# Two transformer stacks on one core: high and low activation parts side by side in one 512-column product

## The chip, the cores and the metric

The kernel runs on one core of one Trainium2 chip, as one program. The metric is the device time of one execution in microseconds. Before the change the median of three runs is 2209.1 us (2205.93 to 2218.09).

## What is computed

The input is one sequence of 256 tokens with 1024 features. Block 1 is two hybrid layers and a final norm, block 2 is two layers with a context of 256 more tokens. Everything is float32.

```python
def hybrid_layer(x, ...):                     # block 1, twice
    h = rms_norm(x, norm_mix)
    proj = h @ w_in                           # 1024 x 10032: all queries, keys, values, gates
    y_nsa, y_sb, y_gla, y_fox = ...           # sparse, stick-breaking, gated linear, forgetting attention
    branch = einsum('bsnc,ncd->bsnd', stack(ys), w_branch)
    gates = sigmoid(gate_logits + b_gate)
    x = x + sum(gates * branch) @ w_out
    h2 = rms_norm(x, norm_ff)
    return x + square(relu(h2 @ w_ff1)) @ w_ff2

# block 2, for each of two layers, modulated by c:
x = layer_norm(alpha * x + g_a * mixer(...))  # layer 0: grouped queries; layer 1: latent attention
x = layer_norm(alpha * x + g_m * square(relu(h @ w1)) @ w2)
```

In the last layer of block 2 only the 256 tokens of x are computed, not the context.

## The kernel before

Activations lie feature by token: x is [128, 8, 256], eight blocks of 128 features by 256 tokens. To keep float32 accuracy with the fast float32r products, each operand is split into a high part (rounded to float32r) and a low part (the rest). A product is then three: high·high, high·low, low·high (mm3, line 348). Weights are loaded by SyncE in tiles of [128, 1024] words (load, 354; five buffers raw), split on ScalarE (cast to hi) and VectorE (subtraction to lo) (split, 359; four buffers each of hi and lo) and used once.

fm8 (372) computes 256 output features for all tokens, a "chunk": for each of two halves of 128 features it loads one weight tile and issues eight triples mm3, k = 0 to 7, with the weights as the stationary operand and 256 columns of xh or xl as the moving one, into one half of a PSUM tile g ([128, 2, 256], one bank, three of them). It is used for the projections of block 1 (16 chunks besides the gates), its gates (16), its output projection (4) and ff1 (16), in each of the two layers. tm8 (381) is the same with tokens as output rows.

layer1 (510) is one layer of block 1. norm_in (721) multiplies x by the norm's gain and splits it into xh and xl; the row scale 1/rms (rc per token, rb broadcast over the partitions) comes later from sumsq (726) and is multiplied in on VectorE as each chunk leaves PSUM (lines 557 to 656, rope 1017) or on ScalarE (tm_evac, 743). branch (569) computes gates and branch projections of one mixer. gla_attn (866) is the gated linear attention: for each half of the tokens t and each pair of heads pr it forms decayed keys xe and queries xq for eight levels and multiplies them per head, with 64 rows of the array (one head has 64 features), into PSUM tiles attps; copy_predicated writes them into att under the masks glm. glq and glk share a tile glqk.

The feed-forward of a layer runs 16 chunks: ff1 (684) with fm8, ReLU, square and split into hid; ff2 (694) adds two rows of 128 hidden features to eight accumulators acc, one chunk behind. When the last row is through, r2b scales each acc and it is added to x. In the second half of the loop of the last layer, at chunk 11, the pool of block 1 on the right side (br) is closed and the one of block 2 opened; context_in (1663) loads the context xc into it and casts its normed parts. VectorE also computes the modulation vectors of block 2 in this loop (ada, 1173).

mlp256 (1518) is the last feed-forward of block 2, on 256 tokens, with the split input hh, hl of two tiles H ([128, 8, 512], of which the tokens use one half); up projection in triples of 256 columns, hidden (1484), and one row of the down projection per step, two steps behind. ln_last (1255) and the output follow.

SBUF has pools on two sides: bp, scp and the weight buffers on the left, br (tags Y, tm, cst and others; for block 2 xc, cst2, H) on the right, where x lies too. Tiles of one tag rotate through its buffers (tag A: 11, tag Y: nY = 3, each of 2048 words per partition). Within a pool the tags lie in the order of their first use.

The order of the instructions on each engine is not the order of the code. The program is built with a planner (TileContext with schedule_with_timeline_sim) that places each instruction by estimated times as its operands and buffers come free. An instruction waits on its engine's queue in that order.

Of the kernel before, what the change touches and what calls it, by code (L numbers as in the profile page):

```python
# [26 lines left out]
BR_ORDER = (1, 2, 0, 3)  # L27

# [278 lines left out]

class Prog:
# [43 lines left out]


# [27 lines left out]
    def tm8(self, src, j, xh, xl):  # L381
# [3 lines left out]
        for t in range(2):  # L385
            s = slice(t * 128, t * 128 + 128)
            for k in range(8):
                h, q = parts[k // 4]
                self.mm3(ps[:, t, :], xh[:, k, s], xl[:, k, s], h[:, k % 4, :], q[:, k % 4, :], k == 0, k == 7)
# [120 lines left out]
    def layer1(self, l):  # L510
# [21 lines left out]
        for j in range(4):  # L532
            h, q = self.split(self.tm_raw[j] if l == 0 else self.load(I[f"wtm{l}"][j], 2, TM_W))
            for t in range(2):
                o = pst[t][:].rearrange("p a b -> p (a b)")[:, :TM_W]
                s = slice(t * 128, t * 128 + 128)
                for k in range(2):
                    kk = j * 2 + k
                    self.mm3(o, xh[:, kk, s], xl[:, kk, s], h[:, k, :], q[:, k, :], kk == 0, kk == 7)
# [16 lines left out]
        for j in range(2):  # L556
            ps = self.fm8(win, C_SBQ + j, xh, xl)
            self.stt(sbq[:, 2 * j:2 * j + 2, :], ps[:], 0.125, rbb, OP.mult, OP.mult)
        for j in range(2):
            ps = self.fm8(win, C_SBK + j, xh, xl)  # L560
            self.tt(sbk[:, 2 * j:2 * j + 2, :], ps[:], rbb, OP.mult)
        for j in range(2):
            self.tm_evac(sbv, j, self.tm8(win, C_SBV + j, xh, xl), rc)
# [1224 lines left out]
```

## Time and profile before

| | us |
|---|---|
| median of three runs | 2209.1 |
| the profiled execution | 2211.48 |
| its span | 2209.8 |
| TensorE busy | 2135.6 (97%) |
| VectorE busy | 1518.5 (69%) |
| ScalarE busy | 1069.7 (48%) |
| GpSimd busy | 132.7 (6%) |

Block 1 takes the first 1211 us or so (layer 0 until about 605), block 2 the rest; mlp256 begins at about 2004 us. TensorE executes 15024 products and as many weight loads. A float32 product that is not float32r is recorded as two passes. Matmuls are pipelined and each row's duration reaches beyond the start of the next, so the price of a product is read from the distance of two starts. In tables of groups the columns are: line, engine, operation, output and inputs by tile names, shape, count, then busy us and mean ns of one, then the idle time before them and what ended it.

### The profile page before, as it was taken

The numbers are of one execution on the slowest core, as the hardware profiler recorded it, in microseconds if no ns is written. First come the engines' busy times: TensorE is split into PE (matmuls) and PEld (weight loads), VectorE is DVE, ScalarE is ACT, GpSimd is POOL, SyncE is SP. The second block draws the span as 40 slices with busy tenths as digits, with TensorE's granted clock in tenths as the row PEclk, the third lists the DMA queues.
The fourth block names the chain that finished last, engine by engine and source line by source line (L and its number), as shares of the span: only waits on it lengthen the run. The fifth ranks groups of instructions, "written<-read, shape, count | busy, mean of one in ns | idle before, by whom it ended". The sixth has DMA issues, their size and how long they took to land. (4 is left out here: it accounts for less than half of the span.)

```text
span 2209.8 us, 37629 instructions
## 1 busy us (share of the span) xinstructions
PE 2135.6 (97%) x15024; PEld 1912.2 (87%) x15024; DVE 1518.5 (69%) x2859; ACT 1069.7 (48%) x1773; POOL 132.7 (6%) x151
## 2 busy tenths in 40 slices
PE   8999999999999999999999899999999999998998
PEld 8889889999998898899999776878888888578997
DVE  6586766788664767677887677479866456756554
ACT  5633554555555335555465477352322325655443
POOL 1100000000001000000000111210000041000000
PEclk9999999999999999999999999999999999999999
DMA  7343334588654433356787110127765322124652
GB/s 264 126 177 117 125 116 159 185 271 275 223 163 125 172 118 127 112 171 188 261 299 235 63 30 29 58 77 219 253 204 178 98 77 76 50 74 132 185 183 77
DMA packets 94388, 335.35 MB, mean 152 GB/s; under 512 B 10722, under 2 KB 12420, under 8 KB 94212
## 3 DMA queue, kind: packets, MB, share of 16 engines
q1 hardware_dynamic: 94212, 332.95, 46.7%
q8 instruction: 118, 1.93, 0.4%
q14 instruction: 58, 0.48, 0.1%
HBM read 331.85 MB, written 1.05 MB: 151 GB/s over the span
## 5 line engine op out<-in xcount | busy, mean ns | idle before, releaser
L321 ACT ACTIVATE hi<-raw 128x1024 fp32r<-128x1024 f32 (+2 forms) x510 | 534.5, 1050 | 754.4 <-PE g L338 242.3
L324 DVE TENSOR_TENSOR lo<-raw,hi 128x1024 fp32r<-128x1024 f32 (+2 forms) x510 | 626.8, 1231 | 312.0 <-ACT hi L321 308.9
L338 PE MATMUL g<-xh,lo 128*128 128x256 f32 x1024 | 294.4, 288 | 0.8 <-DVE lo L324 0.8
L338 PE MATMUL g<-xh,hi 128*128 128x256 f32 x1024 | 295.1, 288 | 0.1
L338 PE MATMUL g<-xl,hi 128*128 128x256 f32 x1024 | 295.1, 288 | 0.0
L338 PE MATMUL acc<-hid,hi 128*128 128x256 f32 x1536 | 278.6, 284 | 2.7 <-ACT hi L321 1.5
L338 PEld LDWEIGHTS acc<-hid,hi 128*128 128x128 f32 x1536 | 237.6, 193 | 3.9 <-ACT hi L321 2.1
L1186 DVE CUSTOM_DVE_ANT_0 sc<-raw,sc 128x1024 f32<-128x1024 f32 x160 | 195.2, 1220 | 49.0 <-DMA raw<-wada 48.7
L338 PE MATMUL acc<-hid,lo 128*128 128x256 f32 x768 | 210.8, 285 | 2.1 <-DVE lo L324 2.0
L338 PEld LDWEIGHTS g<-xh,hi 128*128 128x128 f32 x1024 | 196.3, 192 | 10.4 <-issue 7.9
L338 PEld LDWEIGHTS g<-xl,hi 128*128 128x128 f32 x1024 | 196.2, 192 | 6.4 <-issue 5.5
L338 PEld LDWEIGHTS g<-xh,lo 128*128 128x128 f32 x1024 | 196.4, 192 | 5.3 <-issue 2.7
L338 PE MATMUL gu<-hl,hi 128*128 128x256 f32 (+1 forms) x608 | 196.1, 327 | 1.1 <-DVE hl L332 1.1
L338 PE MATMUL gu<-hh,lo 128*128 128x256 f32 (+1 forms) x608 | 196.2, 328 | 0.5 <-DVE lo L324 0.5
L338 PE MATMUL gu<-hh,hi 128*128 128x256 f32 (+1 forms) x608 | 187.2, 327 | 3.0 <-ACT relu L321 1.9
L338 PEld LDWEIGHTS acc<-hid,lo 128*128 128x128 f32 x768 | 144.7, 193 | 3.6 <-DVE lo L324 3.5
L338 PE MATMUL g<-fh,lo 128*128 128x256 f32 x512 | 145.0, 283 | 0.7 <-DVE lo L324 0.7
L338 PE MATMUL g<-fl,hi 128*128 128x256 f32 x512 | 145.1, 284 | 0.0
L338 PE MATMUL g<-fh,hi 128*128 128x256 f32 x512 | 144.7, 283 | 0.0
L338 PE MATMUL m<-hid,hi 128*128 128x512 f32 x464 | 142.7, 389 | 0.0
L338 PEld LDWEIGHTS gu<-hl,hi 128*128 128x128 f32 x608 | 115.0, 189 | 13.4 <-DVE hl L332 2.1
L338 PEld LDWEIGHTS gu<-hh,lo 128*128 128x128 f32 x608 | 115.0, 189 | 10.9 <-DVE lo L324 0.7
(440 smaller groups left out, 4330.5 us busy)
## 6 DMA issues: line engine op xcount, KB each, us to landing
raw<-win SPq DMA_DIRECT2D x152, 512.0 KB, 3.5
raw<-wff SPq DMA_DIRECT2D x128, 512.0 KB, 4.6
raw<-wada SPq DMA_DIRECT2D x96, 512.0 KB, 4.5
raw<-w1m SPq DMA_DIRECT2D x64, 512.0 KB, 4.3
raw<-w2m SPq DMA_DIRECT2D x64, 512.0 KB, 4.2
raw<-wbr SPq DMA_DIRECT2D x32, 512.0 KB, 3.4
raw<-wc SPq DMA_DIRECT2D x16, 512.0 KB, 3.6
raw<-wout SPq DMA_DIRECT2D x16, 512.0 KB, 3.4
```

The lines of the kernel that those rows point to most:

```text
L321: return self.nc.scalar.activation(out, in_, func, bias=bias, scale=scale)
L324: return self.nc.vector.tensor_tensor(out=out, in0=a, in1=b, op=op)
L338: i = self.nc.tensor.matmul(out, lhsT, rhs, start=start, stop=stop, skip_group_check=True)
L1186: self.nc.vector.tensor_tensor_reduce(out=sc[2][:], in0=w, in1=sc[v][:], op0=OP.mult, op1=OP.add, scale=0.5, scalar=0.0, accum_out=mod[:, ...
```

## The change

A pair tile holds the high and the low part of an activation block next to each other ([128, 4, 2, 256], two tiles of tag Y for all eight blocks). One product of 512 columns then gives weight-high times both parts, and one of 256 columns adds weight-low times the high part to the second half (mm2). The two halves of the PSUM tile are added as they leave (add2: a ScalarE copy of one half, a VectorE addition of the other). fm8 yields one half of 128 features at a time, each in a PSUM tile of its own. This holds for all chunks of block 1 and for the up projection of mlp256.

After the row scale is known a second pair xn = x · gain · rb is formed, and all projections after SBQ and SBK take it, so that the multiplication by rb goes there. In gla_attn the queries of a pair of heads lie side by side in 256 columns with zeros in the other head's rows, so that one product of 128 rows serves both heads; the predicated copies cover both heads too. glk gets a tile of tag Y of its own, nY becomes 5, and the old tiles xh, xl go. The last three rows of the feed-forward's down projection (in both layers of block 1 and in mlp256) run inside one loop over the eight output blocks, so that the accumulators end one after the other. The output projection adds the two halves to x one by one.

```diff
+class Pair:
+    def __init__(self, tiles):
+        self.t = tiles
+    def both(self, k):
+        return self.t[k // 4][:, k % 4]
+    def part(self, j, k, s=slice(0, T)):
+        return self.t[k // 4][:, k % 4, j, s]
+    def two(self, j, k):
+        return self.t[k // 4][:, k % 4:k % 4 + 2, j, :]
...
+    def mm2(self, ps, lh, ll, both, hi, start, stop):
+        self.mm(ps, lh, both, start, False)
+        self.mm(ps[:, 1, :], ll, hi, False, stop)
+    def add2(self, out, ps):
+        self.act(out, ps[:, 1, :])
+        return self.tt(out, out, ps[:, 0, :], OP.add)
...
-    def fm8(self, src, j, xh, xl):
-        ps = self.gtile()
+    def fm8(self, src, j, X):
         for f in range(2):
+            ps = self.gtile()
             h, q = self.split(self.load(src[2 * j + f], 8, 128))
             for k in range(8):
-                self.mm3(ps[:, f, :], h[:, k, :], q[:, k, :], xh[:, k, :], xl[:, k, :], k == 0, k == 7)
-        return ps
...
-        xh = self.bp.tile([128, 8, T], F32R, tag="xh", name="xh", bufs=1)
-        xl = self.bp.tile([128, 8, T], F32R, tag="xl", name="xl", bufs=1)
+        xg = self.pair("xg")
         col = self.psp.tile([128, 512], F32, tag="o", name="ncol", bufs=1)
-        self.norm_in(x, v("gmix"), xh, xl)
+        self.norm_in(x, v("gmix"), xg)
...
-            ps = self.fm8(win, C_SBQ + j, xh, xl)
-            self.stt(sbq[:, 2 * j:2 * j + 2, :], ps[:], 0.125, rbb, OP.mult, OP.mult)
+            s = slice(2 * j, 2 * j + 2)
+            self.fm8_to(sbq[:, s, :], win, C_SBQ + j, xg)
+            self.stt(sbq[:, s, :], sbq[:, s, :], 0.125, rbb, OP.mult, OP.mult)
...
+        xn = self.pair("xn")
+        for k in range(0, 8, 2):
+            t = self.scp.tile([128, 2, T], F32, tag="tmp", name="xnt", bufs=2)
+            for f in range(2):
+                self.stt(t[:, f, :], x[:, k + f, :], v("gmix")[:, k + f:k + f + 1], rb[:], OP.mult, OP.mult)
+            self.act(xn.two(0, k), t[:])
+            self.tt(xn.two(1, k), t[:], xn.two(0, k).bitcast(F32), OP.subtract)
         for j in range(2):
-            self.tm_evac(sbv, j, self.tm8(win, C_SBV + j, xh, xl), rc)
+            self.tm_evac(sbv, j, self.tm8(win, C_SBV + j, xn))
...
-                ps = self.fm8(win, C_GATE + bi * 4 + j, xh, xl)
+                g = gt[-1][:, 2 * (j % 2):2 * (j % 2) + 2, :]
+                for f, ps in self.fm8(win, C_GATE + bi * 4 + j, xn):
+                    self.add2(g[:, f, :], ps)
+                    self.tanh(g[:, f, :], g[:, f, :], hb[:, bi * 8 + 2 * j + f:bi * 8 + 2 * j + f + 1], 0.5)
                 step()
-                g = gt[-1][:, 2 * (j % 2):2 * (j % 2) + 2, :]
-                self.tt(g, ps[:], rbb, OP.mult)
-                for f in range(2):
-                    self.tanh(g[:, f, :], g[:, f, :], hb[:, bi * 8 + 2 * j + f:bi * 8 + 2 * j + f + 1], 0.5)
...
-        glqk = self.a4([128, 2, 2, T], name="glqk")
-        glq, glk = glqk[:, 0], glqk[:, 1]
-        ps = self.fm8(win, C_GLQ, xh, xl)
-        self.stt(glq, ps[:], 0.125, rbb, OP.mult, OP.mult)
-        ps = self.fm8(win, C_GLK, xh, xl)
-        self.tt(glk, ps[:], rbb, OP.mult)
+        glq = self.a4([128, 2, 2, T], name="glq")
+        for h in range(2):
+            nc.gpsimd.memset(glq[64 * (1 - h):64 * (1 - h) + 64, :, h, :], 0.0)
+        tq = self.scp.tile([128, 2, T], F32, tag="tmp", name="glqt", bufs=2)
+        self.fm8_to(tq, win, C_GLQ, xn)
+        for h in range(2):
+            s = slice(64 * h, 64 * h + 64)
+            self.act(glq[s, :, h, :], tq[s], scale=0.125)
+        glk = self.y8([128, 2, T], name="glk")
+        self.fm8_to(glk, win, C_GLK, xn)
...
-        mh = self.y8([128, 8, T], F32R, name="mh")
-        ml = self.y8([128, 8, T], F32R, name="ml")
+        mx = self.pair("mx")
...
-            ps = self.fm8(I[f"wout{l}"], j, mh, ml)
-            self.tt(x[:, 2 * j:2 * j + 2, :], x[:, 2 * j:2 * j + 2, :], ps[:], OP.add)
+            for f, ps in self.fm8(I[f"wout{l}"], j, mx):
+                for e in range(2):
+                    self.tt(x[:, 2 * j + f, :], x[:, 2 * j + f, :], ps[:, e, :], OP.add)
...
-        fh = self.bp.tile([128, 8, T], F32R, tag="xh", name="fh", bufs=1)
-        fl = self.bp.tile([128, 8, T], F32R, tag="xl", name="fl", bufs=1)
+        fx = self.pair("fx")
...
-            ps = self.fm8(I[f"wff1{l}"], ci, fh, fl)
             hid = self.a4([128, 2, 2, T], F32R, name="hid")
             t = self.scp.tile([128, 2, T], F32, tag="tmp", name="relu", bufs=2)
-            self.act(t[:], ps[:], AF.Relu)
+            self.fm8_to(t, I[f"wff1{l}"], ci, fx)
+            self.act(t[:], t[:], AF.Relu)
...
+                if 2 * ci + k < 32 - LAST:
+                    ff2_rows([(2 * ci + k, hid)], lambda f: None)
+        def ff2_rows(rows, done):
+            ws = [(r, hid, self.split(self.load(I[f"wff2{l}"][r], 1, 1024))) for r, hid in rows]
+            for f in range(8):
+                s = slice(f * 128, f * 128 + 128)
+                for r, hid, (h, q) in ws:
+                    self.mm3(acc[f // 2][:, f % 2, :], h[:, 0, s], q[:, 0, s], hid[:, 0, r % 2, :], hid[:, 1, r % 2, :],
+                             r == 0 and f % 2 == 0, r == 31)
+                done(f)
+        def ff_out(f):
+            if f % 2 == 1:
+                j = f // 2
+                t = self.scp.tile([128, 2, T], F32, tag="tmp", name="ffo", bufs=2)
+                self.tt(t[:], acc[j][:], r2bb, OP.mult)
+                self.tt(x[:, 2 * j:2 * j + 2, :], x[:, 2 * j:2 * j + 2, :], t[:], OP.add)
...
+        ff2_rows([(r, hids[r // 2]) for r in range(32 - LAST, 32)], ff_out)
...
+    def pair(self, name):
+        return Pair([self.y8([128, 4, 2, T], F32R, name=name) for _ in range(2)])
...
-                xq = self.a4([128, 8, 128], name="xq")
+                xq = [self.a4([128, 4, 2, 128], name="xq") for _ in range(2)]
                 for hf in range(2):
                     ps = self.psp.tile([128, 512], F32, tag="t", name="eps", bufs=2)
                     w = self.glw[:, t + 4 * hf:t + 4 * hf + 4, :]
...
                     self.mm(ps[:], la_l[:, t, pr * 128:pr * 128 + 128], w, False, True)
                     x4 = slice(4 * hf, 4 * hf + 4)
                     self.act(xe[:, x4, :], ps[:].rearrange("p (a b) -> p a b", a=4), AF.Exp)
-                    self.tt(xq[:, x4, :], xe[:, x4, :], glq[:, pr, ts_].unsqueeze(1).broadcast_to([128, 4, 128]), OP.mult)
+                    self.tt(xq[hf][:], xe[:, x4, :].unsqueeze(2).broadcast_to([128, 4, 2, 128]),
+                            glq[:, pr, :, ts_].unsqueeze(1).broadcast_to([128, 4, 2, 128]), OP.mult)
                 self.tt(xe[:], xe[:], glk[:, pr, ts_].unsqueeze(1).broadcast_to([128, 8, 128]), OP.mult)
-                for lq in range(2):
-                    ps = [self.psp.tile([128, 4, 128], F32, tag="s", name="attps", bufs=2) for _ in range(2)]
-                    for lj in range(4):
-                        li = 4 * lq + lj
-                        for h in range(2):
-                            s = slice(h * 64, h * 64 + 64)
-                            if li == 0:
-                                self.mm(ps[h][:, lj, :], glk[s, pr, ts_], glq[s, pr, ts_])
-                            else:
-                                self.mm(ps[h][:, lj, :], xe[s, slot(li), :], xq[s, slot(li), :])
-                    for lj in range(4):
-                        for h in range(2):
-                            nc.vector.copy_predicated(att[:, 2 * pr + h, :], self.glm[:, 4 * lq + lj, :], ps[h][:, lj, :])
+                for lp in range(4):
+                    ps = self.psp.tile([128, 2, 2, 128], F32, tag="s", name="attps", bufs=2)
+                    for lj in range(2):
+                        li = 2 * lp + lj
+                        if li == 0:
+                            self.mm(ps[:, lj], glk[:, pr, ts_], glq[:, pr, :, ts_])
+                        else:
+                            self.mm(ps[:, lj], xe[:, slot(li), :], xq[slot(li) // 4][:, slot(li) % 4])
+                    for lj in range(2):
+                        nc.vector.copy_predicated(att[:, 2 * pr:2 * pr + 2, :],
+                                                  self.glm[:, 2 * lp + lj, :].unsqueeze(1).broadcast_to([128, 2, 128]),
+                                                  ps[:, lj])
                 if t == 0:
                     self.act(xk0[:, pr, :], xe[:, 0, :])
                 else:
-                    ps = [self.psp.tile([128, 128], F32, tag="s", name="attx", bufs=2) for _ in range(2)]
-                    for h in range(2):
-                        s = slice(h * 64, h * 64 + 64)
-                        self.mm(ps[h][:], xk0[s, pr, :], xq[s, 7, :])
-                    for h in range(2):
-                        self.act(att0[:, 2 * pr + h, 128:256], ps[h][:])
+                    ps = self.psp.tile([128, 2, 128], F32, tag="s", name="attx", bufs=2)
+                    self.mm(ps[:], xk0[:, pr, :], xq[1][:, 3])
+                    self.act(att0[:, 2 * pr:2 * pr + 2, 128:256], ps[:])
...
-            self.nA, self.nY = 11, 3
+            self.nA, self.nY = 11, 5
...
+        def rows(js, done):
+            ws = [(i, hids[i], self.split(self.load(self.i["w2m1"][i], 1, 1024))) for i in js]
+            for f in range(8):
+                w = slice(f * 128, f * 128 + 128)
+                for i, hid, (h, q) in ws:
                     self.mm3(acc[f // 2][:, f % 2, :], h[:, 0, w], q[:, 0, w], hid[:, 0, :T], hid[:, 1, :T],
                              i == 0 and f % 2 == 0, i == 31)
-        for f in range(8):
-            self.stt(X[:, f, s], acc[f // 2][:, f % 2, :], mod[:, 40 + f, 0:1], X[:, f, s], OP.mult, OP.add)
+                done(f)
...
+        def up(ps, k, h, q):
+            self.mm2(ps[:], h[:, k, :], q[:, k, :], hx[:, k], hx[:, k, 0, :], k == 0, k == 7)
...
+            self.add2(t[:, :T], ps)
+            self.stt(t[:, T:], t[:, :T], 0.0, t[:, :T], OP.max, OP.mult)
+            self.act(o[:, 0, :T], t[:, T:])
+            self.tt(o[:, 1, :T], t[:, T:], o[:, 0, :T].bitcast(F32), OP.subtract)
...
+            if 3 <= j < 35 - LAST:
+                rows([j - 3], lambda f: None)
+        rows(range(32 - LAST, 32), out)
...
-            hh, hl = self.w16(name="hh"), self.w16(name="hl")
+            hx = self.w16(name="hx")[:].rearrange("p k (a t) -> p k a t", a=2)
```

## Rows read from the trace of the kernel before

**Rows 1.** The page: busy time by engine; granted TensorE clock in 40 slices.
```profile
PE 2135.6 (97%) x15024; PEld 1912.2 (87%) x15024; DVE 1518.5 (69%) x2859; ACT 1069.7 (48%) x1773; POOL 132.7 (6%) x151
PEclk9999999999999999999999999999999999999999
```
**Rows 2.** Busy time of each engine by stage: stretch, length, then us busy.
```profile
60.00:430.00 370.00, 367.90 (x2871) 334.67 (x2870) 255.39 (x547) 183.17 (x329) 14.46 (x25) 1.00 0.42 139
430.00:603.00 173.00, 171.69 (x1423) 170.79 (x1422) 139.58 (x198) 90.20 (x109) 0.00 (x0) 1.00 0.77 258
...
2016.00:2190.00 174.00, 173.60 (x1448) 173.61 (x1449) 94.37 (x125) 80.23 (x122) 0.00 (x0) 1.00 0.54 167
```
**Rows 3.** TensorE in order of time, a projection: start, length, instruction.
```profile
59.82 0.28 PE L338 MATMUL g<-xh,hi 128*128 128x256 f32 x1
...
60.18 0.28 PE L338 MATMUL g<-xh,hi 128*128 128x256 f32 x1
```
**Rows 4.** TensorE in order of time, the first down projection of block 2.
```profile
1500.05 0.39 PE L338 MATMUL m<-hid,lo 128*128 128x512 f32 x1
...
1500.73 0.39 PE L338 MATMUL m<-hid,lo 128*128 128x512 f32 x1
```
**Rows 5.** TensorE in order of time, the first up projection of block 2.
```profile
1480.07 0.40 PE L338 MATMUL gu<-hh,hi 128*128 128x512 f32 x1
...
1480.77 0.40 PE L338 MATMUL gu<-hh,hi 128*128 128x512 f32 x1
```
**Rows 6.** Groups of instructions: high·high products of the projections and of ff1.
```profile
L338 PE MATMUL g<-xh,hi 128*128 128x256 f32 x1024 | 295.1, 288 | 0.1
...
L338 PE MATMUL g<-fh,hi 128*128 128x256 f32 x512 | 144.7, 283 | 0.0
```
**Rows 7.** Groups of instructions on VectorE and, last, ScalarE.
```profile
L324 DVE TENSOR_TENSOR lo<-raw,hi 128x1024 fp32r<-128x1024 f32 x494 | 612.3, 1241 | 301.3 <-ACT hi L321 298.5 <-PE g L338 0.8
...
L901 DVE COPY_PREDICATED att<-glm,attps 128x128 f32<-128x128 uint8 x128 | 36.6, 300 | 19.3 <-PE attps L338 17.2
...
L324 DVE TENSOR_TENSOR gt<-g,rb 128x512 f32<-128x512 f32 x32 | 21.9, 688 | 10.1 <-PE g L338 9.9
...
L324 DVE TENSOR_TENSOR xq<-xe,glqk 128x512 f32<-128x512 f32 x16 | 10.5, 686 | 0.1
...
L332 DVE SCALAR_TENSOR_TENSOR fnt<-x,lngb,fncol 128x256 f32<-128x256 f32 x8 | 3.6, 476 | 1.8 <-PE fncol L338 1.8
...
L324 DVE TENSOR_TENSOR yns<-nso,yns 128x256 fp32r<-128x256 f32 x8 | 3.4, 425 | 7.2 <-ACT yns L321 7.2
...
L321 ACT ACTIVATE yns<-nso 128x256 fp32r<-128x256 f32 x8 | 3.1, 384 | 10.1 <-PE nso L338 10.1
```
**Rows 8.** TensorE in order of time, two stretches of the gated linear attention.
```profile
144.67 1.71 PE L338 MATMUL attps<-xq,xe 64*128 64x128 f32 x16
...
151.42 0.28 PE L338 MATMUL g<-xh,hi 128*128 128x256 f32 x1
151.62 0.49 PE L338 MATMUL attps<-glqk 64*128 64x128 f32 x2
...
152.93 0.28 PE L338 MATMUL g<-xh,lo 128*128 128x256 f32 x1
```
**Rows 9.** A sum of squares on TensorE: in order of time, and as a group.
```profile
1221.24 1.03 PE L338 MATMUL fncol<-fsq,ones 128*128 128x256 f32 x4
...
L338 PE MATMUL fncol<-fsq,ones 128*128 128x256 f32 x8 | 2.1, 379 | 0.0
```
**Rows 10.** TensorE in order of time, where layer 1 of block 1 begins.
```profile
606.35 0.41 PE L338 MATMUL g<-hi,xh 128*128 128x304 f32 x1 [1.08 <-ACT xh L321]
```
**Rows 11.** The context's tile xc: instructions with first and last start, and landing.
```profile
L321 ACT ACTIVATE ct<-xc,mod x8: 586/587/601, 1149.3 to 1156.7; 128x256 f32<-128x256 f32 x8
...
L1670 SPq DMA_DIRECT2D xc<-ctxT x2: 372/398/424, 1143.9 to 1144.3; - x2
...
DMA to landing us min/median/max: 5.3/6.3/7.4
```

More of the change, by code (lines that the diff above doesn't have):

```diff
@@ L27 @@
 BR_ORDER = (1, 2, 0, 3)
+LAST = 3
 def _cols(w, kt, cw):
@@ L370, in gtile, with fm8_to, tm8 @@
         return self.psp.tile([128, 2, 256], F32, tag="g", name="g", bufs=3)
-    def fm8(self, src, j, xh, xl):
-        ps = self.gtile()
+    def fm8(self, src, j, X):
         for f in range(2):
+            ps = self.gtile()
             h, q = self.split(self.load(src[2 * j + f], 8, 128))
             for k in range(8):
-                self.mm3(ps[:, f, :], h[:, k, :], q[:, k, :], xh[:, k, :], xl[:, k, :], k == 0, k == 7)
-        return ps
-    def tm8(self, src, j, xh, xl):
+                self.mm2(ps[:], h[:, k, :], q[:, k, :], X.both(k), X.part(0, k), k == 0, k == 7)
+            yield f, ps[:]
+    def fm8_to(self, dst, src, j, X):
+        for f, ps in self.fm8(src, j, X):
+            self.add2(dst[:, f, :], ps)
+    def tm8(self, src, j, X):
         ps = self.gtile()
@@ L695, in ff2 @@
             for k in range(2):
[L696 to L702 removed]
+                if 2 * ci + k < 32 - LAST:
[14 more added lines that the diff above has]
+                self.tt(x[:, 2 * j:2 * j + 2, :], x[:, 2 * j:2 * j + 2, :], t[:], OP.add)
+        prev, hids = None, []
         ada = self.ada(0, [self.a4([128, D], name="sc") for _ in range(3)], range(24 * l, 24 * l + 24))
@@ L741, in sumsq, with tm_evac @@
         return self.diag(col, 2)
-    def tm_evac(self, dst, j, ps, rc):
-        for t in range(2):
-            self.act(dst[:, t, j * 256:j * 256 + 256], ps[:, t, :], AF.Identity, scale=rc[:, t:t + 1])
+    def tm_evac(self, dst, j, ps):
+        self.act(dst[:, :, j * 256:j * 256 + 256], ps[:])
     def set_ln(self):
@@ L1516, in mlp512, with mlp256 @@
                         lambda k: (hid[k][:, 0, :], hid[k][:, 1, :]), toks, lambda f, *a: evac(5 + f, *a), done)
-    def mlp256(self, X, hh, hl, mod, s):
+    def mlp256(self, X, hx, mod, s):
         acc = [self.psp.tile([128, 2, T], F32, tag=("s" if j < 2 else "t"), name="acc2", bufs=2) for j in range(4)]
         hids = []
-        first = self.fmu_first([self.i["w1m1"][e] for e in range(3)], hh, hl, [s])
-        for j in range(34):
-            if j < 32:
-                hids.append(self.hidden(first[j] if j < 3 else self.fmu(self.i["w1m1"][j], 8, hh, hl, s), T))
-            if j >= 2:
-                i, hid = j - 2, hids[j - 2]
-                h, q = self.split(self.load(self.i["w2m1"][i], 1, 1024))
-                for f in range(8):
-                    w = slice(f * 128, f * 128 + 128)
+        def rows(js, done):
[3 more added lines that the diff above has]
+                for i, hid, (h, q) in ws:
@@ L1530, in mlp256, with out @@
                     self.mm3(acc[f // 2][:, f % 2, :], h[:, 0, w], q[:, 0, w], hid[:, 0, :T], hid[:, 1, :T],
                              i == 0 and f % 2 == 0, i == 31)
-        for f in range(8):
-            self.stt(X[:, f, s], acc[f // 2][:, f % 2, :], mod[:, 40 + f, 0:1], X[:, f, s], OP.mult, OP.add)
+                done(f)
+        def out(f):
+            if f % 2 == 1:
+                for e in (f - 1, f):
+                    self.stt(X[:, e, s], acc[e // 2][:, e % 2, :], mod[:, 40 + e, 0:1], X[:, e, s], OP.mult, OP.add)
@@ new lines, in mlp256 @@
+        pss = [self.gtile() for _ in range(3)]
+        ws = [self.split(self.load(self.i["w1m1"][e], 8, 128)) for e in range(3)]
+        for k in range(8):
+            for ps, (h, q) in zip(pss, ws):
+                up(ps, k, h, q)
+        for j in range(32):
+            if j < 3:
+                ps = pss[j]
+            else:
+                ps = self.gtile()
+                h, q = self.split(self.load(self.i["w1m1"][j], 8, 128))
+                for k in range(8):
+                    up(ps, k, h, q)
+            hid(ps[:])
+            if 3 <= j < 35 - LAST:
+                rows([j - 3], lambda f: None)
```

70 lines of the change are left out of this document (34 added, 36 removed).

## The prediction, made before the changed kernel ran

> **What bounds the kernel now.** I read the page's busy shares first. TensorE is busy 97% of the span, at full granted clock in every fortieth of it [rows 1]. That share is modelled, so I went to the table by stage. The mixer part of layer 0 (60 to 430 us) has TensorE busy 367.9 of 370 us, its feed-forward part (430 to 603 us) 171.7 of 173, the last MLP (2016 to 2190 us) 173.6 of 174, while VectorE is at 69%, 81% and 54% and ScalarE below that [rows 2]. Layer 1 of block 1 repeats the first two. So in the stages that the change touches only the time that TensorE needs per product counts, unless the edits make another engine late.
>
> The order of TensorE's work then tells the price of one product. In a projection the three products of a triple (256 columns each, each with its own weight load) take 0.36 us, 120 ns each, with no wait between [rows 3]. Products of 512 columns show two prices in the second block. Those of the first down projection, whose moving operand lies in the left-hand pool, take 0.68 us for three, 227 ns each [rows 4]. Those of the up projection, whose moving operand hh lies in the right-hand pool, take 0.70 us for three, 233 ns each [rows 5]. So a product costs its columns and something fixed: two of 256 take 240, one of 512 takes 227 or 233.
>
> **The change part by part.**
>
> *Triples into pairs.* fm8 and the last MLP's up projection issue one 512-column and one 256-column product where three of 256 stood. The columns stay; one weight load and one product go. Block 1 has 1024 + 512 triples in its projections and ff1 [rows 6] and, by the code, 128 in the output projection: 1664. mlp256 has 32 x 8 = 256. The trace has no triple of the new shape, so its price comes from the neighbours: 227 + 120 = 347 ns (13 less than 360) or 233 + 120 = 353 ns (7 less). For block 1 I take 13. The new tiles lie in the right-hand pool as hh does, but hh stands behind a table of 1667 words, so not at a multiple of 16 words, whereas the new tag Y is the first of its pool. That the place and not the side costs the 6 ns is a guess. For mlp256 hx stands where hh stood, so I take 7. Sum: 1664 x 13 = 21.6 us and 256 x 7 = 1.8 us. Bounds of both together: 1920 x 7 = 13.4 us and 1920 x 13 = 25.0 us.
>
> The Trainium skill (TensorE: Matmul & The Clock Gate, Back-to-back issue gap) speaks against this part: it gives the distance of two products as the columns at 2.4 GHz and 2.5 ns more, so a removed product would give back 2.5 ns, by an estimate from that page 4.8 us in all. By that formula 256 and 512 columns would take 109 and 216 ns, and the trace has 120 and 227 or 233, so it doesn't follow it.
>
> *The evacuation.* Each 256-column half now leaves PSUM by a ScalarE copy and a VectorE addition. The nearest rows are y_out's: 384 ns for a copy of 256 from PSUM and 425 ns for an operation on 256 from PSUM; the old multiplication by the row scale over 512 took 688 ns [rows 7]. Where the scale disappears (gates and most projections, 28 of a layer's 52 chunks) VectorE pays 2 x 425 - 688 = 0.16 us more per chunk, in ff1 0.85 (16 chunks), for SBQ and SBK 0.85 (4), in the output projection 4 x 425 - 688 = 1.0 (4): 25.5 us a layer. The new xn adds 8 x 0.476 and 4 x 0.69, 6.6 us. All of it lies beside TensorE's work: 32 us on top of VectorE's 395 busy us in 543 [rows 2] make 79%. Tightest is the feed-forward: 139.6 + 13.6 = 153 of about 170 us, 90%. With that cover gone the price would be all 32 us a layer. ScalarE gains 96 copies of 0.384 = 37 us a layer, on 273 of 543. In mlp256 VectorE pays an operation of 0.476 more per chunk, 15 us on 94 of 174. Each of the three PSUM banks now holds one half instead of two, so TensorE can be 3 x 2.8 = 8 us ahead of an evacuation instead of 17. In ff1 the copy waits behind casts on ScalarE's queue, and the addition then holds up the lo splits behind it on VectorE's. I take 2 us of stalls in all, from 0 to 10. xn hangs on the row scale, but SBQ and SBK (8 halves, 22 us of TensorE) still run on the unscaled pair and cover its 6.6 us.
>
> *Gated pairs.* In the linear attention 64-row products of 128 columns come in groups of eight records, one head at a time. From 151.42 to 152.93 us one group stands between two products of 120 ns: 1.51 - 0.24 = 1.27 us. Two groups joined took 1.71 [rows 8]. Merged, a tile of two levels is four full-row passes of 256 columns. The nearest row, also fp32 with 256 columns, has four in 1.03 us, the last lasting 0.38, so 0.217 each [rows 9]: 0.87 a tile, 0.97 with 0.1 for entering (an estimate). Two groups apart, 2.54 us, become two tiles, 1.94; there are 16 such pairs in both layers, so 9.6 us if all stand apart. Some are joined, and the cross products are halved too, so I take 9. Bounds: 0 (all joined) and 14 (no entering). On VectorE 64 predicated copies of 128 columns at 300 ns go, the other 64 grow to 256 columns (425 by the nearest row): 11 us less. The 16 query products grow from 686 to about 1241: 9 us more [rows 7]. That is even.
>
> *Last rows merged.* At the end of a layer the last accumulators are scaled on VectorE and the next norm follows; TensorE waits 1.08 us for it at 606.35 [rows 10], and about as long for the next operand. With the last three rows interleaved (3 x 24 x 0.12 = 8.6 us) the first accumulator is done 6.5 us before the end instead of 2.2, so 2 us go. But three of four hi and lo buffers stay taken until the end, so the next weights are split late: 0 to 2 us. The end of mlp256 stays, since its additions already ran between the last products.
>
> *A moved wait.* The last layer's fx now lies in the pool that context_in replaces at chunk 11, and is read until chunk 15. The context transfer, issued at 1143.9 us, must now wait for that, when four rows (11.5 us of TensorE) are left. It lands 5.3 to 7.4 us after issue, and its first casts take 7.4 us of ScalarE [rows 11]; block 2 begins with products of them. Its two issues of 512 KB move on SP's queue behind the feed-forward's loads, and block 2's first weights queue behind them. Price 0 to 8 us; I take 2.
>
> Sum, against the profiled execution (2211.5 us, span 2209.8): 2211.5 - 21.6 - 1.8 - 9 - 2 + 2 + 2 = 2181.1. That execution is 2.4 us above the median of 2209.1, so 2179 against the median.
>
> **The rivals.** *Rival 1: the side of the pool sets the price.* Then block 1 saves 7 ns a triple, 11.6 us, and the time is 2189. For it: hh and the new tiles share that side. Against: only the reasoning on places. *Rival 2: the hand-overs give it back.* The context comes 8 us late, the merged pairs bring 2 us, stalls reach 6: 2179 + 6 + 7 + 4 = 2196. For it: every order is laid out anew by a planner that works from estimated times. *Rival 3: a product costs its columns alone.* Then 256 at 120 ns means 512 at 240, the pairs bring nothing, and the time is 2179 + 23.4 = 2202. The 512-column rows speak against it [rows 4, 5]. By the Trainium skill's formula named above (TensorE: Matmul & The Clock Gate, Back-to-back issue gap) it would be 2198, an estimate. *Rival 4, slower: the evacuation becomes the bound.* Each half now needs 0.384 + 0.425 us on two queues in turn, ahead of later splits. If TensorE waits for that, it pays up to 0.81 us on each of 224 halves (64 each in gates, other projections and ff1, 32 in mlp256). It decides from 0.20 us a half on: 44 us, the gain of 33 and 11 more. At 0.4 us, half the chain, on the 128 halves of gates and ff1, the time is 2179 + 51 = 2230. For it: VectorE at 90% in the feed-forward. Against: VectorE now idles 298 us before its lo splits, waiting for casts [rows 7], and splits run ahead by four buffers.
>
> **How the numbers follow.** Forecast 0.55, rival 1 0.17, rival 2 0.15, rival 3 0.05, rival 4 0.08. A measurement of this kernel tells about 0.5% from no change: 2198 to 2220. Faster: 0.55 + 0.17 + half of rival 2 = 0.79. Same: the other half and rival 3 = 0.13. Slower: 0.08. The range: at the low end all pairs at 13 ns (1.6), 14 us from the attention (5), no stalls and no late context (4) and boundaries 2 us better, 2179 - 13 = 2166; at the high end rival 3, 2203. Rival 4 stays out.
>
> **What would show it.** The starts of g's 512-column products, 227 or 233 ns to the next, settle rival 1; one pair must sum to 347 or 353 ns. The matmul records should fall by 1920 and about 136, VectorE gain about 75 us, TensorE stay full in the stages. TensorE idle behind an addition or copy from g would be rival 4; a wait at block 2's first gk products behind xc the moved wait. The prediction is wrong if the feed-forward stretches don't shorten by about 3.3 us each.

## The result: slower, and where the time went

The changed kernel took 2233.7 us at the median against 2208.1 for the kernel before: a ratio of 1.0113, 95% interval 1.0091 to 1.0135. The prediction, 2179 us and faster, was wrong in sign, and the time lies outside its range. The profiled execution took 2232.9 us, its span 2231.1.

The page after, busy time by engine and granted clock (as [rows 1]):

```profile
PE 2118.0 (95%) x12968; PEld 1800.9 (81%) x12968; DVE 1574.7 (71%) x3011; ACT 1136.6 (51%) x1968; POOL 139.7 (6%) x155
...
PEclk9989999999999999999999899999999999998999
```

TensorE has 2056 records less, as forecast (1920 and 136), but its share of the span fell from 97 to 95%, and three slices of the clock row are below 9. Span less busy time is TensorE's idle time: 74.2 us before (2209.8 - 2135.6), 113.1 after (2231.1 - 2118.0). So the busy time fell by 17.6 us (pairs and attention stand in the forecast's sum with 32.4), and the idle time rose by 38.9: the difference is the 21 us by which the span grew. The stages (as [rows 2]; busy us of PE, PEld, DVE, ACT and POOL, then the granted clock):

```profile
60.00:438.00 378.00, 362.28 (x2272) 302.49 (x2270) 258.86 (x558) 201.25 (x382) 19.75 (x27) 0.98 0.45 139
438.00:622.00 184.00, 177.75 (x1220) 163.06 (x1220) 153.01 (x236) 100.37 (x141) 0.46 (x1) 0.99 0.74 239
2043.00:2213.00 170.00, 170.00 (x1212) 159.73 (x1211) 105.44 (x154) 77.43 (x117) 1.47 (x2) 1.00 0.51 166
```

In the mixer part TensorE now lacks 15.7 us where it lacked 2.1, in the feed-forward 6.2 where it lacked 1.3; only the last MLP stays full. VectorE is busy 83% of the feed-forward, so by its share it is not the bound.

For the runs below I cut the span at the starts of named products: the last of ncol (sum of squares of a layer's first norm), the first of scps (scores of the sparse attention), the last of fcol (sum of squares of the norm ahead of the feed-forward), the last of acc, the first of gq (queries of block 2). Lengths in us, one profiled execution each; the last two rows are the time in which TensorE is idle in such stretches, both layers together. Since each kernel's order is laid out anew, some work moves across a cut: in r_after one half of ff1 (2.8 us) lies ahead of fcol's last product in each layer.

| stretch | before | after | three_keep | ff1_three | r_after | gt_tag | comb5 | before_gla |
|---|---|---|---|---|---|---|---|---|
| layer 0, ncol to scps | 185.5 | 198.4 | 191.5 | 196.4 | 194.7 | 194.0 | 192.0 | 183.2 |
| layer 0, scps to fcol | 219.5 | 214.8 | 220.5 | 215.2 | 212.0 | 213.3 | 209.8 | 217.9 |
| layer 0, fcol to end of acc | 176.2 | 185.8 | 183.0 | 180.0 | 176.6 | 186.2 | 178.0 | 178.3 |
| layer 1, ncol to scps | 186.9 | 191.9 | 187.0 | 190.4 | 191.4 | 186.0 | 184.7 | 182.5 |
| layer 1, scps to fcol | 218.0 | 214.1 | 219.7 | 214.4 | 210.7 | 213.6 | 207.0 | 217.9 |
| layer 1, fcol to gq of block 2 | 212.1 | 219.3 | 216.0 | 209.0 | 211.9 | 218.2 | 209.8 | 211.2 |
| last MLP, acc | 172.2 | 169.3 | 170.8 | 168.2 | 168.2 | 168.2 | 168.2 | 172.2 |
| idle, ncol to scps | 3.7 | 26.0 | 11.9 | 25.0 | 16.4 | 9.2 | 6.1 | 5.4 |
| idle, fcol to end of acc | 5.5 | 19.9 | 14.9 | 6.0 | 15.4 | 20.0 | 4.5 | 5.8 |

After against before: +12.9 and +5.0 ahead of scps, +9.6 and +7.2 in and behind the feed-forwards, -4.7, -3.9 and -2.9 where TensorE stayed the bound; with -2.1 in the stretches not shown this is the 21 us of the spans. Three places make up most of the losses.

**The feed-forward.** What SyncE's queue, which issues the loads, waited for in the first feed-forward (us, times, longest), before and after:

```profile
SPq L356 <- DVE lo L324: 88.5, 44, 5.7
```

```profile
SPq L393 <- DVE relu L352: 55.8, 24, 3.0
...
SPq L393 <- DVE lo L352: 26.2, 19, 2.5
```

Already before, a load waited until a lo split gave its raw buffer back; five buffers go round. After, the additions (relu) stand in that way. The total of these waits is no price: it was 88.5 us before, when TensorE lost next to nothing. It tells which engine a load hangs on. VectorE, SyncE, ScalarE and TensorE in one chunk of after:

```profile
463.03 0.41 DVE L352 TENSOR_TENSOR relu<-relu,g 128x256 f32<-128x256 f32 x1
463.37 1.22 DVE L352 TENSOR_TENSOR lo<-raw,hi 128x1024 fp32r<-128x1024 f32 x1
464.50 0.41 DVE L352 TENSOR_TENSOR relu<-relu,g 128x256 f32<-128x256 f32 x1
464.83 1.22 DVE L1245 CUSTOM_DVE_ANT_0 sc<-raw,sc 128x1024 f32<-128x1024 f32 x1
...
465.98 2.35 DVE L352 TENSOR_TENSOR lo<-raw,hi 128x1024 fp32r<-128x1024 f32 x2
...
467.22 7.86 SPq L393 DMA_DIRECT2D raw<-wff  x4
...
472.41 1.06 ACT L349 ACTIVATE hi<-raw 128x1024 fp32r<-128x1024 f32 x1 [3.52 <-DMA raw<-wff]
...
473.52 0.74 PE L366 MATMUL acc<-hid,hi 128*128 128x256 f32 x4 [0.83 <-ACT hi L349]
```

The second addition and the work behind it put off the pair of splits at 465.98; the next load is issued at 467.22, when the first of them is done; the cast waits 3.5 us for a transfer, and TensorE for the cast. Gaps of 0.75 to 1.8 us at this place, from the start of g's last product to that of acc's first, come in five chunks of layer 0 and as often in layer 1. The Trainium skill (Perfetto Trace Analysis, Optimization Strategy) says that a gap that repeats on the engine that should be full can mean too little SBUF or PSUM for the next tile. The runs agree: with six raw buffers throughout (raw6, below) these gaps are gone.

**The linear attention.** ScalarE, then TensorE, and the stretch in sixths:

```profile
141.66 1.08 ACT L349 ACTIVATE xe<-eps 128x512 f32<-128x512 f32 x2 [5.04 <-PE eps L366]
142.76 1.28 ACT L349 ACT_TABLE_LOAD   x1
153.20 1.06 ACT L349 ACTIVATE silu<-glg 128x1024 f32<-128x1024 f32 x1 [9.16 <-PE attps L366]
155.02 0.94 ACT L349 ACTIVATE gt<-g 128x256 f32<-128x256 f32 x3 [0.76 <-PE attps L366]
```

```profile
126.64 0.27 PE L366 MATMUL g<-xn,lo 128*128 128x256 f32 x1
...
156.99 0.50 PE L366 MATMUL g<-xn,hi 128*128 128x512 f32 x1 [0.27 <-DVE gt L352]
```

```profile
130.00:136.00 6.00, 3.45 (x16) 2.03 (x16) 4.42 (x9) 1.05 (x3) 0.00 (x0) 0.79 0.83 302
136.00:142.00 6.00, 5.80 (x28) 3.66 (x28) 3.19 (x6) 0.95 (x3) 0.00 (x0) 0.64 0.52 171
...
148.00:154.00 6.00, 5.07 (x13) 3.54 (x12) 2.64 (x7) 0.80 (x1) 0.00 (x0) 0.50 0.19 70
```

Three gate halves fill g's three banks at 126.9 us and stay until 155. Their copies stand behind silu on ScalarE's queue, and silu itself waits 9.2 us, until a product of attps. By the code both write tiles of the tag A, of which a pass now holds three instead of two, so I take it that they wait for a slot; gt_tag below tests this. For 30 us TensorE has no gate products to put between the passes; it stands in between, and part of the time runs at half clock.

**The rotated projections.** The copies of the last of three projections out of PSUM wait until VectorE has finished the first rotation (kr) and with it left one of the two buffers of rraw; scps waits 3.7 us for the rotated queries nq of the second. ScalarE, then TensorE (the same 3.7 us again in layer 1):

```profile
220.09 0.66 ACT L349 ACTIVATE rraw<-g 128x256 f32<-128x256 f32 x2 [2.71 <-DVE kr L352]
```

```profile
220.71 0.63 PE L366 MATMUL scps<-kcbd,nq 128*128 128x32 f32 x4 [3.72 <-DVE nq L352]
```

### The profile page after: what moved, and what is told of

It reads as the page before. It is cut to its first block, busy times and chain, and to the rows that moved or that the text cites. A ratio compares the mean times of both kernels' runs of the same rounds, so it can differ in the third digit from the quotient of the medians.

```text
span 2231.1 us, 33911 instructions
## 1 busy us (share of the span) xinstructions
PE 2118.0 (95%) x12968; PEld 1800.9 (81%) x12968; DVE 1574.7 (71%) x3011; ACT 1136.6 (51%) x1968; POOL 139.7 (6%) x155
## 4 chain that ended last, share of the span: by engine, by line
PE 77%; DVE 10%; DMA 6%; ACT 4%; issue 3%; POOL 0%; SPq 0%; POOLq 0%; ACTq 0%; DVEq 0%
PE g L366 33%; PE gu L366 8%; PE acc L366 7%; PE m L366 7%; DMA raw<-wff 5%; DVE lo L352 3%; PE py L366 2%; PE gq L366 2%; PE pt L374 2%; ACT hi L349 2%; PE o L366 2%; DVE sc L1245 2%; PE sps L366 1%; PE attps L366 1%; PE sm L366 1%
## 5 line engine op out<-in xcount | busy, mean ns | idle before, releaser
L366 PE MATMUL g<-xn,hi 128*128 128x512 f32 x896 | 327.6, 405 | 0.3 <-DVE gt L352 0.3
L366 PE MATMUL g<-xn,lo 128*128 128x256 f32 x896 | 256.4, 286 | 0.0
L366 PEld LDWEIGHTS g<-xn,hi 128*128 128x128 f32 x896 | 169.6, 189 | 44.3 <-issue 6.3
L366 PE MATMUL g<-fx,hi 128*128 128x512 f32 x512 | 184.9, 399 | 3.8 <-DVE relu L352 2.1
L366 PEld LDWEIGHTS g<-xn,lo 128*128 128x128 f32 x896 | 170.5, 190 | 5.2 <-issue 3.3
L366 PE MATMUL g<-fx,lo 128*128 128x256 f32 x512 | 140.8, 281 | 1.5 <-DVE lo L352 1.5
L366 PE MATMUL gu<-hl,hi 128*128 128x512 f32 (+1 forms) x352 | 123.9, 359 | 0.7 <-DVE hl L360 0.7
L366 PE MATMUL gu<-hh,lo 128*128 128x512 f32 (+1 forms) x352 | 124.4, 361 | 0.0
L366 PE MATMUL gu<-hh,hi 128*128 128x512 f32 (+1 forms) x352 | 117.0, 360 | 1.0 <-ACT relu L349 1.0
L366 PEld LDWEIGHTS m<-hid,hi 128*128 128x128 f32 x464 | 87.1, 188 | 18.2
L366 PEld LDWEIGHTS g<-fx,lo 128*128 128x128 f32 x512 | 96.7, 189 | 3.8 <-DVE lo L352 2.7
```

Source lines behind the costliest of these rows:

```text
L366: i = self.nc.tensor.matmul(out, lhsT, rhs, start=start, stop=stop, skip_group_check=True)
```

## The experiments

Ratios are to the kernel before on the same chip, with a 95% interval; a difference of two kernels in us is that of their ratios, times 2209.

**three_keep**: is it the pair?

```diff
-        self.mm(ps, lh, both, start, False)
+        self.mm(ps[:, 0, :], lh, both[:, 0, :], start, False)
+        self.mm(ps[:, 1, :], lh, both[:, 1, :], False, False)
```

> The changed kernel with its tiles and evacuations, but each pair of products (512 and 256 columns) is issued as three of 256 again, into the same halves. Theory A, a pair saves 7 ns where TensorE sets the time, that is in the projections, the output projection and the last MLP: 1408 times 7 is 10 us, and the feed-forward, which the splits set, does not change: 2242 to 2246. Rival B, a pair saves as much everywhere: 1920 times 7 is 13 us, 2247. Rival C, the pair brings nothing: 2234.

Measured 1.0114 (1.0099 to 1.0129), rival C. Its page, span 2233.1 us:

```profile
PE 2137.1 (96%) x14888; PEld 1905.2 (85%) x14888; DVE 1574.7 (71%) x3011; ACT 1138.3 (51%) x1968; POOL 136.3 (6%) x155
```

TensorE's busy time is 19.1 us more than in the changed kernel and its idle time 17.1 less (96.0 against 113.1): what the pairs save there comes back as waiting. By the table, from scps to fcol, where TensorE is the bound, it lost 5.7 us in each layer; in the other four stretches of block 1 it gained 18. Why these came out shorter, and not merely as long, is open.

**ff1_three** takes the pairs out of ff1:

```diff
-            self.fm8_to(t, I[f"wff1{l}"], ci, fx)
-            self.act(t[:], t[:], AF.Relu)
+            ps = self.gtile()
...
+                    self.mm3(ps[:, f, :], h[:, k, :], q[:, k, :], fx.part(0, k), fx.part(1, k), k == 0, k == 7)
+            self.act(t[:], ps[:], AF.Relu)
```

> The changed kernel, but ff1 computes three products of 256 columns into one bank again and Relu reads that bank, so ff1's copies and additions (64 each in the two layers) are gone; all else stays. Theory A, the copies and additions delay the lo splits on VectorE and with them the reuse of the raw buffers: the feed-forward stretches, from the first to the last product of acc, fall from 183 and 190 us to at most 177 and 184, and the kernel by 12 to 18 us, to 2216 to 2222. Rival B, something else in the stage makes it longer (the merged last rows, the clock): the stretches stay within 3 us and the kernel stays at 2230 to 2238, since ff1's pairs of products, 512 times 7 ns, are given back too.

Measured 1.0032 (1.0012 to 1.0051), 2216.1 us: A, 18 us. From fcol to the end of acc TensorE idles 6.0 us instead of 19.9.

**r_after**, after raw6, a kernel with six raw buffers throughout (1.0010, 0.9994 to 1.0026; feed-forwards shorter by 16 and 14 us, block 2 longer by 18 for the room it gave up):

```diff
+        if self.in1 and self.nload % 6 == 0:
+            raw = self.bp.tile([128, 1024], F32, tag="rawx", name="raw", bufs=1)
```

> The changed kernel with a sixth raw buffer in block 1 alone (every sixth load there takes it; room made by pi, lf and hv in the tag A), block 2 as it was. In raw6 the feed-forward stretches fell by 15.9 and 14.3 us, while two P2 buffers instead of three cost block 2 18 us. If the loads that wait for a raw buffer are what ff1's additions lengthen: the same stretches fall by 10 to 16 us each and the kernel by 20 to 32, to 2202 to 2214, ratio 0.997 to 1.002. If raw6 gained by its other edits: within 8 us of the changed kernel.

Measured 1.0008 (0.9990 to 1.0027), 23 us less. The feed-forwards fell by 9.2 and 7.4 us, under the forecast, and 2.8 us of each is work moved across the cut; the rest came elsewhere in block 1. Its loads in the first feed-forward wait 31.9 us behind additions instead of 55.8, but 60.8 behind splits instead of 26.2:

```profile
SPq L399 <- DVE lo L352: 60.8, 30, 10.9
...
SPq L399 <- DVE relu L352: 31.9, 20, 2.9
```

What TensorE waited for in the first feed-forward of the changed kernel, of r_after, and, all its waits from 430 to 615 us, of raw6:

```profile
PE acc L366 <- ACT hi L349: 4.6, 5, 1.5
```

```profile
PE g L368 <- ACT hi L349: 4.3, 6, 1.0
...
PE acc L368 <- ACT hi L349: 0.4, 1, 0.4
```

```profile
PE acc L366 <- ACT hid L349: 1.1, 1, 1.1
PE g L366 <- DVE xg L360: 1.1, 1, 1.1
PE g L366 <- DVE lo L352: 0.7, 1, 0.7
```

In raw6, with every addition still there, no wait for a weight cast (hi) is left in it; over both feed-forwards these waits fall from 12.2 us to 0.9. So it is by the raw buffers that the additions hold TensorE up. In r_after, where only every sixth load takes the new buffer, 10.1 us of them stay; most of the idle time that it saves lies ahead of scps (16.4 us instead of 26.0).

**gt_first** allocated gt ahead of the passes:

> The changed kernel, but the two gate tiles of the first branch are allocated ahead of the linear attention, which now has four slots of the tag A for its passes instead of six. Theory A, TensorE starves in the linear attention because the gate halves fill all three PSUM banks and have no slot to be evacuated to (each pass takes three slots instead of two): gate products stand between the passes again, the first product of scps comes at 208 to 213 us instead of 220.7, and the kernel falls by 10 to 18 us, to 2216 to 2224. Rival B, the chain of a pass on VectorE (7 us, four passes) sets the stage: no gain, or up to 10 us slower, since passes overlap less: 2232 to 2244.

Measured 1.0120 (1.0104 to 1.0135), but it tells nothing of the two: the planner gives slots in its own order, and the first gate copy stayed at 154.1 us.

**gt_tag** does it with a tag:

```diff
-                    gt.append(self.a4([128, 4, T], name="gt"))
+                    gt.append(self.bp.tile([128, 4, T], F32, tag="G", name="gt", bufs=2))
-            self.nA, self.nY = 11, 5
+            self.nA, self.nY = 9, 5
```

> The changed kernel, but the gate tiles gt have two slots of their own and the tag A has nine instead of eleven, so that the room is the same and a gate half can be evacuated while the linear attention holds its slots (in gt_first the planner gave the slots to the passes all the same). Theory A, in the linear attention TensorE stands because three gate halves fill PSUM and can't leave it before 155 us: gate products stand between the passes, the first product of scps comes at 205 to 212 us and 815 to 825 us instead of 220.7 and 832.3, and the kernel falls by 8 to 20 us, to 2214 to 2226. Rival B, the chain of the passes on VectorE sets the stage and with four slots for them they overlap less: scps no earlier, 2232 to 2245.

Measured 1.0049 (1.0031 to 1.0067), 14 us less: A, though scps came at 216.3 us in layer 0, less early than A said (822.4 in layer 1). TensorE idles 9.2 us ahead of scps instead of 26.0. Gate copies begin at 120 us, and TensorE is full at full clock:

```profile
130.00:136.00 6.00, 6.00 (x35) 4.67 (x34) 4.79 (x9) 1.84 (x3) 0.00 (x0) 1.00 0.43 116
...
148.00:154.00 6.00, 6.00 (x35) 4.89 (x35) 5.15 (x9) 3.20 (x6) 0.00 (x0) 1.00 0.46 143
```

rope_a (rraw in the tag A) gave 1.0091 (1.0058 to 1.0124): no clear gain; the wait ahead of scps fell from 3.7 to 0.5 us, and one of 3.5 us of g took its place.

**comb3** is ff1_three, gt_tag and rope_a together, and **comb5** lets the rotated projections leave one bank in one copy:

```diff
-        self.fm8_to(raw, src, j, X)
+        ps = self.gtile()
...
+                self.mm3(ps[:, f, :], h[:, k, :], q[:, k, :], X.part(0, k), X.part(1, k), k == 0, k == 7)
+        self.nc.vector.tensor_copy(raw[:], ps[:])
```

> The three edits ff1_three, gt_tag and rope_a together in the changed kernel. If the slowdown is made of places where a half can't leave PSUM in time, the gains add up: 17.6 from ff1 and 10 to 25 from the other two, 2190 to 2206, faster than the kernel before (2208). If another wait takes their place: 2206 to 2216.

> comb3, but the three rotated projections are computed with three products into one bank and leave it by one copy on VectorE. Theory A, the 3.8 us waits at 201 and 800 us come from the second rotated projection, whose halves can't leave PSUM until VectorE has done the first rotation: both go, 5 to 8 us less than comb3, ratio to before 0.992 to 0.993. Rival B, VectorE's queue there holds any evacuation up: within 2 us of comb3.

comb3 measured 0.9958 (0.9941 to 0.9974): the gains add up, as forecast (2203.6 us). comb5 measured 0.9926 (0.9907 to 0.9944), 2194.4 us: faster than the kernel before and the changed one. It is 7 us less than comb3, as A said, though the two intervals overlap; the waits of g there (2.7 and 3.1 us) are gone, and one of 2.0 us of rps has come in each layer. Its page, span 2192.2 us, idle time 82.3:

```profile
PE 2109.9 (96%) x13576; PEld 1828.0 (83%) x13576; DVE 1552.2 (71%) x2941; ACT 1113.4 (51%) x1892; POOL 139.5 (6%) x155
```

**comb3_three** is comb3 with three_keep's edit:

> comb3 with each pair of products issued as three of 256 again (tiles and evacuations stay). In the changed kernel that edit cost nothing. Theory A, there the pair's saving went into the waits for evacuations, and in comb3, where these waits are mostly gone, it counts: slower than comb3 by 7 ns times 1408 triples (ff1 has three in both), 10 us, ratio to before 1.000 against 0.996. Rival B, a pair saves nothing that counts in any of these kernels: within 3 us of comb3.

Measured 1.0060 (1.0037 to 1.0083), 22 us slower than comb3: with the waits mended the pairs pay. The pages of comb3 (span 2201.4 us) and comb3_three (2219.6):

```profile
PE 2114.3 (96%) x13480; PEld 1828.9 (83%) x13480; DVE 1553.8 (71%) x2947; ACT 1114.9 (51%) x1904; POOL 140.8 (6%) x155
```

```profile
PE 2132.7 (96%) x14888; PEld 1909.4 (86%) x14888; DVE 1550.6 (70%) x2947; ACT 1119.4 (50%) x1904; POOL 137.2 (6%) x155
```

The idle time is the same, 87.1 and 86.9 us, and the busy time 18.4 more: 13 ns for each of 1408 pairs, where A had taken 7.

The other parts. **before_gla**, the merged linear attention alone:

> The kernel before, with the linear attention of the changed one alone (merged pairs, three slots a pass, glk in a tile of its own). The prediction's term: 9 us less than before, ratio 0.996, within 0 to 14. Rival, the third slot a pass makes TensorE wait for room in the tag A: 0 to 10 us slower, ratio 1.000 to 1.0045.

Measured 0.9997 (0.9982 to 1.0011): between -4.0 and +2.4 us, so not the 9, and of the rival only its low end is left. In its profile the stretches that hold it are 2.3 and 4.4 us shorter, and TensorE is busy 7.1 us less in the span (2128.5 against 2135.6). That the median shows none of it goes with the granted clock: the median of its runs is 0.988, that of the kernel before beside them 0.992. At 0.989 four of its runs took 2204 to 2209 us, the kernel before 2211 and 2213 at 0.990. Why it was granted less is open. gla_old, the changed kernel with the attention as before, gave 1.0060 (1.0035 to 1.0085), so there the merging cost about 12 us, though scps came no earlier without it (221.6 us). comb5 with the old attention gave 0.9916 (0.9895 to 0.9938), not told from comb5: no gain from the merging in any median.

**fx_left** keeps the last layer's fx in the left pool:

> The changed kernel, but the last layer's fx lies in four slots of the left pool, so the context's load needn't wait for the last product of ff1. Theory A, the moved wait costs its 4.1 us and up to 3 us of low clock after it: the kernel falls by 4 to 7 us, to 2227 to 2230. Rival B, the load comes earlier but its three transfers of 0.5 MB and the casts of the context take the room of the last feed-forward chunks, or the four slots are missed by hid: within 2 us of 2234.

Measured 1.0136 (1.0121 to 1.0151): no gain, so not A. The context now comes 48 us earlier, its casts stand ahead of ff1's cast on ScalarE's queue, and TensorE waits there:

```profile
1185.41 0.49 PE L377 MATMUL g<-fx,hi 128*128 128x512 f32 x1 [3.38 <-ACT hi L360]
```

In comb5 the same edit gave 0.9913 (0.9893 to 0.9933), not told from comb5.

**comb5_seq** undoes the merged last rows:

> comb5, with the last three rows of the down projections one after the other again, in block 1 and in the last MLP (the earlier LAST = 1 left out row 30 of each layer and rows 29 and 30 of the last MLP, so it says nothing). The prediction gave the merging 2 us and nothing at the end of the last MLP. If so: 1 to 3 us slower than comb5. Rival, the held buffers take it back: within 1.5 us.

Measured 0.9931 (0.9909 to 0.9953), not told from comb5 either; its last MLP lasts the same 168.2 us. (LAST = 1 took 2196 us in comb3, but left out rows, as said above.)

**r_pair**, comb5 with ff1's pairs and the sixth buffer:

> comb5 with ff1's pairs, copies and additions back (as in the changed kernel) and the sixth raw buffer in block 1. If the buffer covers the additions, ff1's pairs pay their 512 times 7 to 10 ns: 2 to 8 us less than comb5, ratio 0.989 to 0.992. If the additions still hold up the splits: 5 us or more slower than comb5.

Measured 0.9973 (0.9957 to 0.9989), 10 us slower than comb5: the additions still hold up the splits. In its feed-forwards TensorE waits 11.3 us for weight casts, in comb5 1.5, as in r_after, whose way of giving every sixth load the new buffer it shares. comb5 with the pairs and raw6's six buffers was not tried.

## Why the prediction was wrong, step by step

*The step that failed* is the evacuation: "I take 2 us of stalls in all, from 0 to 10." In its place the runs showed 38.9 us more of TensorE's idle time. Mending the three places took 30.8 of them away again and gave 41 us (1.0113 to 0.9926), though the mending also undoes 608 of the 1920 pairs. By the prediction's own sign the feed-forward stretches were to become 3.3 us shorter; that of layer 0 became 9.6 longer. The prediction named the pieces, one half in each bank, the copy behind casts, the addition ahead of splits, and weighed them by VectorE's share (90%) and by four hi and lo buffers. It followed the split on to TensorE, not back to the raw buffer and the load. Its evidence against rival 4, that VectorE idles 298 us before its splits, holds for the average; the view that speaks against it, the waits of SyncE's queue (88.5 us on lo splits in one feed-forward: the loads already hung on VectorE), was not read. Rival 4's price, 2230 us, is near the result, in part by luck: its 0.4 us a half was half of a chain, assumed. Its place is right only in part: gates and ff1 as it said, but through slots, queues and loads, not because an engine was full. It got a chance of 0.08.

*Pairs.* The price was nearly right. The plain rule gave 347 ns, rival 1 353; a stretch of the rotated projections:

```profile
204.75 0.39 PE L366 MATMUL g<-xn,hi 128*128 128x512 f32 x1
204.99 0.28 PE L366 MATMUL g<-xn,lo 128*128 128x256 f32 x1
...
206.14 0.39 PE L366 MATMUL g<-xn,hi 128*128 128x512 f32 x1
```

four pairs in 1.39 us, 347 each, against 360 for a triple [rows 3]. Over all pairs of xn the median distances are 233 and 117 ns, 350 a pair: the 512-column product costs what hh's cost [rows 5], so the guess on places was wrong and rival 1 right in that (that the side of the pool is the reason isn't shown), but the product behind it takes 117, not 120. A pair saves 10 to 13 ns (13 between comb3 and comb3_three), and rival 3 is out. Only where TensorE remained the bound did it reach the span: -4.7 and -3.9 us there.

*Gated pairs.* 9 us were forecast; no median shows them, and in the changed kernel the merging cost 12. On TensorE the price was not far off: 7.1 us less busy in before_gla. The VectorE side was sized right: 440 ns for a predicated copy (425 taken) and 1218 for a query product (1241). The sum left out the third slot that a pass takes; that this slot, and not another part of the merging, costs the 12 us isn't shown.

*Last rows.* 2 us were forecast; comb5_seq can't tell 2 us from none. *Moved wait.* Its place was right, and its size too small:

```profile
1227.85 0.58 PE L366 MATMUL gk<-hh,hi 128*128 128x256 f32 x1 [4.11 <-ACT hh L349]
```

4.1 us against 2, inside its bounds; xc is issued at 1219.5 us, after ff1's last product (1219.16). But in fx_left, without that wait, another came. *xn*: hidden by SBQ and SBK, as said; TensorE is busy 36.0 of the 36 us from 24 to 60. *VectorE* gained 56 us instead of 75.

*The sum, mended.* 2177 us without stalls (the forecast less its 2), plus 9 and 2 for the terms of which no median shows anything, plus 608 pairs of 13 ns, 7.9, is 2196 (with 10 ns a pair in block 1, 2199); comb5 measured 2194. That is no proof of each term: comb5 idles 8 us more than the kernel before (82.3 against 74.2), which this sum puts at nothing, so the nearness is in part luck.

## What to carry to other kernels

Before a change puts work on the engine that frees the load buffers, read what the load queue waits for: if it waits for that engine, an operation ahead of the freeing one can delay a transfer, however idle the engine is on average. The total of such waits doesn't price it; what TensorE waits for does. When a product's result grows, so that a bank holds half as much, ask for each consumer where it goes, in which queue, and whether its target has a free slot; a busy share answers none of that. And a saving on the busiest engine counts only in the stretches that it bounds, so sum it by stretch.

## What the hardware did that was not expected

After its stalls TensorE ran for a while at the lower clock, 1.2 GHz: the granted clock is 0.50 from 148 to 154 us, and TensorE had stood for 1.4 us up to 145.7 and for 0.9 us up to 147.2. In the feed-forward it is 0.52 from 488.4 to 491 us. The distance of two products there:

```profile
489.70 0.63 PE L366 MATMUL acc<-hid,lo 128*128 128x256 f32 x2
490.13 0.63 PE L366 MATMUL acc<-hid,hi 128*128 128x256 f32 x2
```

two in 0.43 us, 213 to 215 ns each, the 256 columns at 1.2 GHz and nothing more, while at 2.4 GHz it is 120 (107 for the columns). And a pair at 0.50, in fx_left:

```profile
1187.39 0.63 PE L377 MATMUL g<-fx,hi 128*128 128x512 f32 x1
1187.82 0.41 PE L377 MATMUL g<-fx,lo 128*128 128x256 f32 x1
1188.03 0.63 PE L377 MATMUL g<-fx,hi 128*128 128x512 f32 x1
```

0.64 us, as much as three of 213 ns. So what a pair saves is there only at the full clock. The Trainium skill (TensorE: Matmul & The Clock Gate, Back-to-back issue gap) gives for the gap of single products the columns alone at the lower clock, with which this agrees, and 2.5 ns more at the full one, where the trace has 13. The kernel before had such stretches too (0.76 from 1106 to 1112 us), but the mean granted clock of the profiled execution fell from 0.989 to 0.983. The runs of the kernel before beside before_gla took 2206 to 2207 us at 0.994 and 2213 to 2218 at 0.986; by that an estimate gives the 0.006 some 4 to 9 us of the 21. So the clock is part of the loss. That it follows the stalls is argued from the order, and from gt_tag, where it stays at 1.00 without them.
